# Value and output-gate projections with 512 moving columns, and half of the transposed inputs in another buffer

## The chip, the cores and the metric

The kernel runs on one core of one Trainium2 chip. The metric is device microseconds per execution: the median of three runs, beside one profiled execution whose trace is read here. A core has engines that run their own queues of instructions in order and wait for each other by semaphores: TensorE (PE, with its weight loads shown as PEld), VectorE (DVE), ScalarE (ACT), GpSimd (POOL) and SyncE (SP), which here only issues DMA transfers.

## The reference

One layer of a streaming encoder, in float32, for 2048 prompt frames (in chunks of 64 for the recurrence) and 64 sample frames that continue a running stream; model width 1024.

```
mod = silu(c) @ w_ada + b_ada                       # shift, scale, gate, twice
hn = rms(x) * (1 + sc1) + sh1
q, f, iv, og, xr, gr = split(hn @ w_in)             # six parts of 512 columns
o = hgrn2(silu(q), log(fgate(f)), 1 - fgate(f), iv) # 4 heads of 128, gated linear recurrence
o_hg = o * rsqrt(mean(o*o)) * gain * silu(og)       # og: the output gate
o_rg = rglru(conv4(xr)) * gelu(gr)                  # real-gated recurrence
x = x + g1 * (concat(o_hg, o_rg) @ w_out)
hn2 = rms(x) * (1 + sc2) + sh2
x = x + g2 * (relu(hn2 @ w_up)**2 @ w_down)         # d_ff = 4096
y = rms(x) * final_gain
```

`iv` are the values and `og` the output gate of the four HGRN2 heads. Final states are outputs too.

## The kernel before

**Blocks.** The prompt is worked in 4 blocks of 512 frames; the last block takes the 64 sample frames along (`B.last`). Activations are kept transposed (model width on the partitions) in `B.XT`, as a high part in a rounded 32-bit format and a low part with the rest; a weight tile `wt` also has a high and a low half of 1024 columns each. Each product is three matmuls: high x high, high x low, low x high.

**Weights.** A "unit" is 128 x 1024 numbers of a weight matrix. In block 0 a unit of `w_in` or `w_out` is loaded raw by SyncE, cast by ScalarE (L244), its rest is taken by VectorE or GpSimd (L245), and the split tile of 1 MB is written to memory; blocks 1 to 3 load that kept tile by GpSimd's queue (L263). `w_up` and `w_down` are split afresh in each block. All split tiles live in one pool `wp` of six slots, taken in the order of the program text; raw ones in `rawp`, of three.

**One block**, in the order of the text: the projections of head 0 (`hg_proj`, ps_in), the values (`hg_vo(B, 0)`), the gates (`hg_vo(B, 1)`), the projections of the other heads, with the recurrence of each head (`hg_chunks`: ps_dg, ps_lv, ps_kT, ps_dS, ps_o; then, in the second part, the norm, the gate and the transposes ps_oT) between them; the recurrent branch (`rg_in`, `rg_scan`, `rg_out`); the output projection (`phase_O`, ps_y); then eight groups of the MLP, up (`phase_U`, ps_u) and down. A scheduler writes the order of each engine's queue at compile time, by the rank that `sec(...)` gives a part and by its own estimate of when operands are ready. In `sec`, the last up group has rank 180, the next block's `phase_A` 182, the down group 6 185, the down group 7 195.

**hg_vo.** The activations are the stationary operand (128 frames), the weights move. For each of two halves of 256 columns, two units of 256 columns each cover the 8 slices of the model width; for each tile of 128 frames 24 matmuls sum into `ps_vo`, and ScalarE or VectorE write the result to `B.vo`. Head h reads columns 128 h to 128 h + 127 of it: ps_dS the values, L900 the gates. Value tiles of a head are needed for all four tiles of 128 frames before the head's state sums.

**phase_A** of the next block runs while the last groups of the MLP do. It spreads the frames' row scales over the partitions by four matmuls (ps_rs), copies them to an `hd` tile (L531, 512 of its 2560 columns), loads the transposed input in four quarters (`x_t`, 512 KB each), scales them with VectorE (L538), and writes XT (L539 by ScalarE, L540 by VectorE). XT has one buffer, so this waits for the last up group's matmuls. Quarters 0 and 1 live in `xap`, quarters 2 and 3 in the pool `rowp` (two buffers, tag "row").

**Down projection of blocks 1 to 3** (`phase_W`, ps_d): seven products of half-size blocks take the place of eight; the weight combinations are made on the way, from four raw tiles (`down_units`), two of them in the same pool "row":

```
r11, r21 = load_raw(w_down[u]), load_raw(w_down[u + 1])
r12, r22 = (rowp.tile([P, 1028], F32, tag="row", name="raw")[:, :D] for _ in range(2))
Q.dma_start(r12, w_down[u + 2])
Q.dma_start(r22, w_down[u + 3])
```

Four subtractions (L1036) and seven splits (L244 and L245) follow; the first two products need only r11 and r21. The left factors (gA, gS) are sums of the up result, made by VectorE in `sums_of` (L965 to L974) from an `hd` tile; each product's two results are added to accumulators by VectorE (L1086), and `combine` (L1115) puts them together after group 7. Block 0 uses the plain `phase_D0` (L1063).

The pools that the change touches: `hdp` has 2 buffers of 2560 columns, `rowp` 2, `xap` 2, `wp` 6.

Of the kernel before, what the change touches and what calls it, by code (L numbers as in the profile page):

```python
# [9 lines left out]
F32 = mybir.dt.float32  # L10
# [3 lines left out]
AF = mybir.ActivationFunctionType  # L14
# [5 lines left out]
P = 128  # L20
D = 1024
KD = 8
# [35 lines left out]
IN_UNIT = list(range(24))  # L58
# [23 lines left out]
def layout(inputs):  # L82

    a = {k: np.ascontiguousarray(v) for k, v in inputs.items()}
    d = {k: a[k] for k in ("x_prompt", "x_sample", "state_hgrn", "final_gain")}
    names = ("c_prompt", "c_sample", "b_ada", "conv_w", "conv_b", "rg_ba", "rg_bx", "rg_lambda",
             "hg_lb_logits", "hg_norm_gain", "cache_conv", "state_rglru")
    a["b_ada"] = a["b_ada"].reshape(6, D)[PARTS]
    rows = np.concatenate([a[k].reshape(-1, P) for k in names])
    small = np.zeros((P, P), np.float32)  # L90
    small[:, :len(rows)] = rows.T
    d["small"] = small

    def cols(w, n):
        return w.reshape(KD, P, -1, n).transpose(2, 1, 0, 3)

    xt = a["x_prompt"][0].reshape(-1, BLK, 4, 2, P)

    gate_w = np.zeros((P, 4, 2, P), np.float32)
    for m, nm in enumerate(("rg_wa", "rg_wx")):  # L100
        for c in range(4):
            for hf in range(2):
                sl = slice(hf * 64, hf * 64 + 64)
                gate_w[sl, c, m, sl] = a[nm][0][2 * c + hf]
    d["rg_w"] = gate_w.reshape(P, D)
    d["x_t"] = np.ascontiguousarray(xt.transpose(0, 2, 4, 3, 1)).reshape(-1, 4, P, 2 * BLK)
    win = a["w_in"][0]
    units = []
    for c in range(0, 24):
        if 8 <= c < 16:  # L110
            if c % 2 == 0:
                u = cols(win[:, c * P:(c + 2) * P], 256)[0]
                units += [u[:, 0:4].reshape(P, 1024), u[:, 4:8].reshape(P, 1024)]
        else:
            units.append(cols(win[:, c * P:(c + 1) * P], P)[0].reshape(P, 1024))
    d["w_in"] = np.stack(units)
    d["w_up"] = np.ascontiguousarray(cols(a["w_up"][0], P)).reshape(DFF // P, P, 1024)
    d["w_out"] = np.ascontiguousarray(
        a["w_out"][0].reshape(4, 2, P, 2, 512).transpose(3, 0, 2, 1, 4)).reshape(8, P, 1024)
    d["w_down"] = np.ascontiguousarray(  # L120
        a["w_down"][0].reshape(8, 2, 2, P, 2, 512).transpose(0, 4, 1, 3, 2, 5)).reshape(32, P, 1024)
    wa = a["w_ada"][0].reshape(KD, P, 6, KD, P)
    d["w_ada1"] = np.ascontiguousarray(wa[:, :, 0:2].transpose(3, 1, 0, 2, 4)).reshape(KD, P, KD, 2 * P)
    d["w_ada2"] = np.ascontiguousarray(wa[:, :, PARTS[2:]].transpose(2, 0, 1, 3, 4)).reshape(4, KD, P, D)
    d["ident"], d["masks"] = consts()
    return d
# [3 lines left out]
def hymba_step(ctx: ExitStack, tc: tile.TileContext, i: dict, o: dict):  # L130
# [335 lines left out]
    def rows(tok):  # L466


        return P if tok[2] else tok[1]
# [26 lines left out]
                          reason="late load")  # L496


    def x_load(src, n, after, row=False):
        x = rowp.tile([P, 1028], F32, tag="row", name="x_a")[:, :D] if row else xap.tile([P, D], F32, tag="xa", name="x_a")  # L500
        d = Q.dma_start(x[:n], src)
        if after is not None:
            gate(d, after)
        return x
# [10 lines left out]
    def phase_A(B, after=None):  # L515


        B.XT = Split(xtp, "xt", KD, "XT1")
        if B.last:
            n = LS  # L520
            x = x_load(xs, n, after)
            hd = hdp.tile([P, 2560], F32, tag="hd", name="hd_a")
            rs = rms_rstd(x, hd[:, :D], n)
            V.tensor_scalar(x[:n], x[:n], rs[:n, 0:1], None, op0=ALU.mult)
            norm_T(x, hd[:, 0:D], B.XT, BLK, n, 1, SC1, SH1)
        hd = hdp.tile([P, 2560], F32, tag="hd", name="hd_a")
        ps = pax.tile([P, 512], F32, tag="ax", name="ps_rs")
        for t in range(4):
            T.matmul(ps[:, t * P:(t + 1) * P], lhsT=B.rs[:, t:t + 1].to_broadcast([P, P]), rhs=ident, start=True, stop=True)
        rb = hd[:, 0:BLK]  # L530
        S.copy(rb, ps)  # L531
        for k2 in range(4):
            x = x_load(i["x_t"][B.b, k2], P, after, k2 > 1).rearrange("p (k t) -> p k t", k=2)
            for kk in range(2):
                k = 2 * k2 + kk
                sc, sh = modc[:, SC1, 0, k:k + 1], modc[:, SH1, 0, k:k + 1]
                hi, lo = (y[:, k, :BLK] for y in B.XT.p)
                V.scalar_tensor_tensor(x[:, kk], x[:, kk], sc, rb, op0=ALU.mult, op1=ALU.mult)  # L538
                S.activation(hi, x[:, kk], AF.Identity, bias=sh)  # L539
                V.scalar_tensor_tensor(lo, x[:, kk], sh, hi.bitcast(F32), op0=ALU.add, op1=ALU.subtract)  # L540
# [211 lines left out]
    def hg_vo(B, m):  # L752
        if m == 0:
            B.vo = [vop.tile([P, 2, 512], F32, tag="vo", name="vo") for _ in B.toks]
            B.rgw = vop.tile([P, 4, 2, P], F32, tag="vo", name="rgw")
            Q.dma_start(B.rgw.rearrange("p c m n -> p (c m n)"), i["rg_w"])
            if B.last:
                B.Ss = vop.tile([P, 2 * NH, P], F32, tag="vo", name="Sst_s")[:, :NH]
                Q.dma_start(B.Ss, i["state_hgrn"][0, 0].rearrange("h d v -> d h v"))
        for hf in range(2):  # L760
            c0 = (2 + m) * 512 + hf * 256
            ws = [unit(w_in, IN_UNIT[c0 // P] + u, 256, (EV if B.b else EV0)[u], "in", B.b) for u in range(2)]
            for ti, (t0, n, which, _, _) in enumerate(B.toks):
                ps = pmu.tile([P, 512], F32, tag="mu", name="ps_vo")
                ops = [(k, l, a) for k in range(KD) for l, a in passes(B.toks[ti], B.XT, k)]
                for q, (k, l, a) in enumerate(ops):
                    T.matmul(ps[:rows(B.toks[ti]), :256], lhsT=l, rhs=ws[k // 4][:, a, k % 4],  # L767
                             start=(q == 0), stop=(q == len(ops) - 1))
                dst = B.vo[ti][:n, m, hf * 256:hf * 256 + 256]
                if which:  # L770
                    halves(dst, ps[:, :256], n, which)
                    if m:
                        S.activation(ps[:n, :256], dst, AF.Sigmoid)
                        V.tensor_mul(dst, dst, ps[:n, :256])
                elif m == 0:
                    B.iv = S.copy(dst, ps[:n, :256])
                else:
                    S.activation(dst, ps[:n, :256], AF.Sigmoid)
                    B.og = V.tensor_mul(dst, dst, ps[:n, :256])

    def hg_group(B, tile_, n, C, which):
        g = Block()
# [556 lines left out]
```

## Time and profile before

| | |
|---|---|
| median of 3 runs | 2690.6 us (2690.57 to 2698.39) |
| profiled execution | 2700.03 us, span 2698.3 us |
| granted TensorE clock, mean | 0.955 |
| TensorE busy | 2493.6 us, 92% |
| VectorE busy | 1817.2 us, 67% |
| ScalarE busy | 1043.5 us, 39% |
| GpSimd busy | 188.0 us, 7% |

Shares are means over the span. Successive matmuls overlap, so a group's busy time divided by its number is longer than the distance between the starts of two matmuls; that distance is read from the timeline, as the time from the start of a row to the start of the next one divided by the number of matmuls in the row. VectorE instructions overlap by some 0.08 us in the same way.

### The profile page before, as it was taken

The page shows a single profiled execution, that of the slowest core. Times are in us where ns is not written, and L with a number is a line of the kernel's source. Part 1 is how long each engine was busy: PE and PEld are TensorE (multiplying, and loading weights), DVE is VectorE, ACT ScalarE, POOL GpSimd, SP SyncE. Part 2 cuts the span into 40 slices and gives each one's busy share as a digit, 9 for nine tenths or more (in the row PEclk, how much of TensorE's full clock was granted, in tenths as well). Part 3 has the DMA queues.
Part 4 walks back from the last instruction along what each step waited for, and adds up shares of the span by engine and source line. Part 5 has one row for each costly group of instructions (what it writes and reads, how often), then busy time and mean ns, then how long its engine had stood idle before and what let it go on. Part 6 is the DMA issues. An engine that isn't in the chain of part 4 may idle for free.

```text
span 2698.3 us, 34804 instructions
## 1 busy us (share of the span) xinstructions
PE 2493.6 (92%) x13592; PEld 2129.3 (79%) x13592; DVE 1817.2 (67%) x3267; ACT 1043.5 (39%) x1683; POOL 188.0 (7%) x245
## 2 busy tenths in 40 slices
PE   5878899999899999999799989999789998999997
PEld 4866787887797778888587878888579877998976
DVE  7676675766554656878864656778773576568787
ACT  4234152223212446445312436445411624644432
POOL 2311100000011100000001100000010110000000
PEclk8888799999999999999899999999889999999998
DMA  8563555667353542234363442234253643222223
GB/s 332 219 227 132 202 182 187 211 210 242 126 203 124 180 141 78 94 110 156 113 223 125 180 140 79 94 109 153 93 207 110 149 126 129 79 78 92 81 68 109
DMA packets 96420, 397.44 MB, mean 147 GB/s; under 512 B 14432, under 2 KB 16384, under 8 KB 79360
## 3 DMA queue, kind: packets, MB, share of 16 engines
q1 hardware_dynamic: 79696, 274.63, 29.6%
q0 software_dynamic: 16560, 120.59, 12.9%
q8 instruction: 107, 1.75, 0.3%
q14 instruction: 57, 0.47, 0.0%
HBM read 343.77 MB, written 51.41 MB: 146 GB/s over the span
## 4 chain that ended last, share of the span: by engine, by line
PE 70%; DVE 14%; issue 7%; DMA 5%; ACT 3%; POOL 1%; SPq 0%; DVEq 0%; POOLq 0%; ACTq 0%
PE ps_u L1011 24%; PE ps_d L1097 15%; PE ps_in L649 7%; PE ps_vo L767 6%; PE ps_d L1063 6%; PE ps_y L937 3%; DMA raw<-in_w_ada_dram 2%; PE ps_lv L841 2%; DVE wt L245 2%; PE ps_in L634 1%; PE ps_rg L710 1%; DVE ada_acc L333 1%; PE ps_s L1107 1%; PE ps_ada L337 1%; DMA wt<-kept_out 1%
## 5 line engine op out<-in xcount | busy, mean ns | idle before, releaser
L1011 PE MATMUL ps_u<-XT,wt 128*128 128x512 f32 (+2 forms) x4128 | 746.5, 341 | 17.1 <-ACT XT L399 5.9
L1011 PEld LDWEIGHTS ps_u<-XT,wt 128*128 128x128 f32 x4128 | 656.0, 189 | 99.4 <-ACT XT L399 7.1
L245 DVE TENSOR_TENSOR wt<-raw,wt 128x1024 fp32r<-128x1024 f32 x338 | 414.9, 1240 | 237.6 <-ACT wt L244 206.1
L244 ACT CAST wt<-raw 128x1024 fp32r<-128x1024 f32 x357 | 371.4, 1048 | 331.4 <-PE ps_d L1063 93.1
L649 PE MATMUL ps_in<-XT,wt 128*128 128x512 f32 (+1 forms) x1776 | 377.7, 363 | 12.9 <-ACT wt L244 6.6
L649 PEld LDWEIGHTS ps_in<-XT,wt 128*128 128x128 f32 x1776 | 293.0, 191 | 60.3 <-ACT wt L244 8.5
L1097 PE MATMUL ps_d<-wt,gS 128*128 128x512 f32 x1104 | 269.0, 402 | 41.0 <-ACT wt L244 30.7
L1097 PEld LDWEIGHTS ps_d<-wt,gS 128*128 128x128 f32 x1104 | 212.8, 194 | 92.8 <-ACT wt L244 32.3
L937 PE MATMUL ps_y<-wt,mix 128*128 128x512 f32 x800 | 207.1, 413 | 13.6 <-DVE hd_o L942 5.1
L1014 ACT ACTIVATE hd_u<-ps_u 128x512 f32<-128x512 f32 (+2 forms) x172 | 85.2, 498 | 344.3 <-PE ps_u L1011 341.0
L767 PE MATMUL ps_vo<-wt,XT 128*128 128x256 f32 x1600 | 212.6, 289 | 2.6 <-POOL wt L245 1.7
L767 PEld LDWEIGHTS ps_vo<-wt,XT 128*128 128x128 f32 x1600 | 201.0, 195 | 3.9 <-POOL wt L245 1.9
L1097 PE MATMUL ps_d<-wt,gA 128*128 128x512 f32 x828 | 196.9, 390 | 0.2
L937 PEld LDWEIGHTS ps_y<-wt,mix 128*128 128x128 f32 x800 | 154.8, 198 | 53.0 <-DVE hd_o L942 6.4
L1063 PE MATMUL ps_d<-wt,gt 128*128 128x512 f32 x768 | 182.2, 398 | 8.3 <-DVE acc L1068 8.3
L1097 PEld LDWEIGHTS ps_d<-wt,gA 128*128 128x128 f32 x828 | 154.7, 188 | 33.0 <-DVE wt L245 1.0
L1063 PEld LDWEIGHTS ps_d<-wt,gt 128*128 128x128 f32 x768 | 147.9, 193 | 40.1 <-DVE acc L1068 8.7
L1036 DVE TENSOR_TENSOR raw<-raw 128x1024 f32<-128x1024 f32 x92 | 113.4, 1233 | 4.3 <-DMA raw<-in_w_down_dram 2.2
L841 PEld LDWEIGHTS ps_lv<-hd_h 128*128 128x128 f32 x640 | 88.9, 211 | 24.6 <-issue 15.6
L1086 DVE TENSOR_TENSOR acc<-acc,ps_d 128x512 f32<-128x512 f32 x160 | 106.5, 680 | 1.9 <-PE ps_d L1097 0.9
L841 PE MATMUL ps_lv<-hd_h 128*128 128x64 f32 x640 | 92.3, 292 | 14.5 <-DVE hd_h L846 9.0
L1086 DVE TENSOR_TENSOR accM<-accM,ps_d 128x512 f32<-128x512 f32 x120 | 79.7, 681 | 38.5 <-PE ps_d L1097 38.1
(306 smaller groups left out, 2671.1 us busy)
## 6 DMA issues: line engine op xcount, KB each, us to landing
wt<-kept_in POOLq DMA_DIRECT2D x72, 1024.0 KB, 6.8
raw<-in_w_up_dram SPq DMA_DIRECT2D x128, 512.0 KB, 4.3
raw<-in_w_down_dram SPq DMA_DIRECT2D x128, 512.0 KB, 3.5
raw<-in_w_ada_dram SPq DMA_DIRECT2D x80, 512.0 KB, 4.8
wt<-kept_out POOLq DMA_DIRECT2D x24, 1024.0 KB, 5.2
kept_in<-wt POOLq DMA_DIRECT2D x19, 1024.0 KB, 8.8
raw<-in_w_in_dram SPq DMA_DIRECT2D x24, 512.0 KB, 5.3
x_a<-in_x_prompt_dram SPq DMA_DIRECT2D x16, 512.0 KB, 5.3
```

What stands on the lines that cost most here:

```text
L244: S.copy(wt[:, 0], raw)
L245: eng.tensor_tensor(wt[:, 1], raw, wt[:, 0].bitcast(F32), op=ALU.subtract)
L649: T.matmul(ps[:, :pn], lhsT=w[:, a, k], rhs=B.XT.p[x][:, k, p0:p0 + pn], start=(k == 0 and q == 0), stop=(k == KD - 1 and q == 2))
L767: T.matmul(ps[:rows(B.toks[ti]), :256], lhsT=l, rhs=ws[k // 4][:, a, k % 4], start=(q == 0), stop=(q == len(ops) - 1))
L841: T.matmul(ps[:C, c * C // 2:(c + 1) * C // 2].rearrange("p (b h) -> p b h", h=hs), lhsT=KS[:, c * C:c * C + C], rhs=qv[:, c * bc:(c + 1) ...
L937: T.matmul(ps[:rows(B.toks[ti])], lhsT=l, rhs=ws[k - k % 2][:, a, k % 2], start=(q == 0), stop=(q == len(ops) - 1))
L1011: T.matmul(ps[:, :pn], lhsT=w[:, a, k], rhs=B.XT.p[x][:, k, p0:p0 + pn], start=(k == 0 and q == 0), stop=(k == KD - 1 and q == 2))
L1014: S.activation(r, ps[:, :pn], AF.Relu)
L1036: V.tensor_tensor(d, x, y, op=ALU.subtract)
L1063: T.matmul(ps, lhsT=l, rhs=ws[half][c // 2][:, a, c % 2], start=(q == 0), stop=(q == len(ops) - 1))
L1086: return V.tensor_tensor(dst, dst, ps, op=ALU.add)
L1097: T.matmul(ps, lhsT=op[x][y][:, c, t * P:(t + 1) * P], rhs=w[:, a, c], start=(k == 0), stop=(k == len(ops) - 1))
```

## The change

`hg_vo` no longer goes over two halves: four units, each with 512 columns of two slices of the model width, are taken at once, and each tile of 128 frames is 24 matmuls of 512 columns into a whole `ps_vo`. The evictions are as wide. `layout` packs the units to match; their number and size stay. In `phase_A` the four quarters are asked for before the copy of the row scales, and quarters 2 and 3 go to columns 512 to 1535 and 1536 to 2559 of the `hd` tile that holds the row scales, no longer to "row".

```
     for c in range(0, 24):
         if 8 <= c < 16:
-            if c % 2 == 0:
-                u = cols(win[:, c * P:(c + 2) * P], 256)[0]
-                units += [u[:, 0:4].reshape(P, 1024), u[:, 4:8].reshape(P, 1024)]
+            if c % 4 == 0:
+                u = cols(win[:, c * P:(c + 4) * P], 512)[0]
+                units += [u[:, k:k + 2].reshape(P, 1024) for k in range(0, KD, 2)]
...
-    def x_load(src, n, after, row=False):
-        x = rowp.tile([P, 1028], F32, tag="row", name="x_a")[:, :D] if row else xap.tile([P, D], F32, tag="xa", name="x_a")
+    def x_load(src, n, after, x=None):
+        if x is None:
+            x = xap.tile([P, D], F32, tag="xa", name="x_a")
...
         rb = hd[:, 0:BLK]
+        xts = [x_load(i["x_t"][B.b, k2], P, after, hd[:, k2 * D - 1536:k2 * D - 512] if k2 > 1 else None) for k2 in range(4)]
         S.copy(rb, ps)
         for k2 in range(4):
-            x = x_load(i["x_t"][B.b, k2], P, after, k2 > 1).rearrange("p (k t) -> p k t", k=2)
+            x = xts[k2].rearrange("p (k t) -> p k t", k=2)
...
-        for hf in range(2):
-            c0 = (2 + m) * 512 + hf * 256
-            ws = [unit(w_in, IN_UNIT[c0 // P] + u, 256, (EV if B.b else EV0)[u], "in", B.b) for u in range(2)]
-            for ti, (t0, n, which, _, _) in enumerate(B.toks):
-                ps = pmu.tile([P, 512], F32, tag="mu", name="ps_vo")
-                ops = [(k, l, a) for k in range(KD) for l, a in passes(B.toks[ti], B.XT, k)]
-                for q, (k, l, a) in enumerate(ops):
-                    T.matmul(ps[:rows(B.toks[ti]), :256], lhsT=l, rhs=ws[k // 4][:, a, k % 4],
-                             start=(q == 0), stop=(q == len(ops) - 1))
-                dst = B.vo[ti][:n, m, hf * 256:hf * 256 + 256]
...
+        u0 = IN_UNIT[8 + 4 * m]
+        ws = [unit(w_in, u0 + u, 512, (EV if B.b else EV0)[u % 2], "in", B.b) for u in range(4)]
+        for ti, (t0, n, which, _, _) in enumerate(B.toks):
+            ps = pmu.tile([P, 512], F32, tag="mu", name="ps_vo")
+            ops = [(k, l, a) for k in range(KD) for l, a in passes(B.toks[ti], B.XT, k)]
+            for q, (k, l, a) in enumerate(ops):
+                T.matmul(ps[:rows(B.toks[ti])], lhsT=l, rhs=ws[k // 2][:, a, k % 2],
+                         start=(q == 0), stop=(q == len(ops) - 1))
+            dst = B.vo[ti][:n, m]
...
```

The lines left out write `dst` from `ps` as before, with 512 columns in place of 256.

## Rows read from the trace of the kernel before

**Rows 1.** The page, part 1: engine, busy us, share of the span, instructions.

```profile
PE 2493.6 (92%) x13592; PEld 2129.3 (79%) x13592; DVE 1817.2 (67%) x3267; ACT 1043.5 (39%) x1683; POOL 188.0 (7%) x245
```

**Rows 2.** TensorE's timeline from block 1 to 2.

```profile
1269.58 21.92 PE L1011 MATMUL ps_u<-XT,wt 128*128 128x512 f32 x96
1291.34 1.05 PE L529 MATMUL ps_rs<-ident,rsq 128*128 128x128 f32 x8
1292.15 5.72 PE L1097 MATMUL ps_d<-wt,gA 128*128 128x512 f32 x24
1311.68 12.51 PE L1097 MATMUL ps_d<-wt,gS 128*128 128x512 f32 x42 [13.81 <-ACT wt L244]
...
1345.64 8.33 PE L1097 MATMUL ps_d<-wt,gS 128*128 128x512 f32 x24 [3.58 <-DVE acc L1086]
...
1356.53 11.04 PE L649 MATMUL ps_in<-XT,wt 128*128 128x512 f32 x48
```

**Rows 3.** Windows: us, busy of PE, PEld, DVE, ACT, POOL, clock, DMA share, GB/s.

```profile
1269.00:1292.00 23.00, 23.00 (x106) 19.15 (x105) 8.02 (x9) 7.71 (x11) 0.00 (x0) 1.00 0.27 92
1292.00:1356.00 64.00, 45.10 (x170) 34.00 (x169) 60.08 (x79) 22.12 (x29) 2.64 (x5) 0.81 0.46 160
...
1879.00:1902.00 23.00, 23.00 (x108) 18.80 (x107) 9.98 (x20) 8.73 (x14) 0.00 (x0) 1.00 0.26 92
1902.00:1970.00 68.00, 46.02 (x175) 34.88 (x175) 62.29 (x85) 24.07 (x35) 1.85 (x4) 0.80 0.39 133
```

**Rows 4.** The page, part 5: the group of the value and gate matmuls.

```profile
L767 PE MATMUL ps_vo<-wt,XT 128*128 128x256 f32 x1600 | 212.6, 289 | 2.6 <-POOL wt L245 1.7
```

**Rows 5.** TensorE's timeline, block 1: start us, us, what, idle before.

```profile
786.69 14.88 PE L767 MATMUL ps_vo<-wt,XT 128*128 128x256 f32 x122
801.52 0.33 PE L904 MATMUL ps_oT<-ident,hd_h 128*128 128x128 f32 x1
...
810.85 7.55 PE L767 MATMUL ps_vo<-wt,XT 128*128 128x256 f32 x61
818.24 14.92 PE L649 MATMUL ps_in<-XT,wt 128*128 128x512 f32 x65
```

**Rows 6.** Timelines of TensorE and VectorE at the three block changes.

```profile
712.51 40.13 PE L1063 MATMUL ps_d<-wt,gt 128*128 128x512 f32 x168 [8.25 <-DVE acc L1068]
...
1267.93 0.68 DVE L965 TENSOR_TENSOR gS<-hd_u,gS 128x512 fp32r<-128x512 f32 x1
...
1905.21 0.42 DVE L400 TENSOR_TENSOR XT<-hd_a,XT 128x256 fp32r<-128x256 f32 x1
...
1912.38 0.74 DVE L538 SCALAR_TENSOR_TENSOR x_a<-x_a,modc,hd_a 128x512 f32<-128x512 f32 x1
...
1925.47 1.65 PE L1097 MATMUL ps_d<-wt,gS 128*128 128x512 f32 x3 [16.86 <-ACT wt L244]
```

**Rows 7.** SyncE's timeline around both changes; L1032, L1033 load r12, r22.

```profile
1250.32 3.96 SPq L501 DMA_DIRECT2D x_a<-in_x_t_dram  x2
...
1271.67 2.56 SPq L250 DMA_DIRECT2D raw<-in_w_down_dram  x3
1305.66 0.33 SPq L1032 DMA_DIRECT2D raw<-in_w_down_dram  x1
1308.84 0.33 SPq L1033 DMA_DIRECT2D raw<-in_w_down_dram  x1
...
1919.59 0.33 SPq L1032 DMA_DIRECT2D raw<-in_w_down_dram  x1
```

**Rows 8.** VectorE's groups in 1292 to 1356: count, busy us, mean ns.

```profile
L245 DVE TENSOR_TENSOR wt<-raw,wt 128x1024 fp32r<-128x1024 f32 x12 | 14.2, 1217 | 0.5 <-ACT wt L244 0.5
...
L1036 DVE TENSOR_TENSOR raw<-raw 128x1024 f32<-128x1024 f32 x8 | 9.7, 1217 | 0.0
```

**Rows 9.** Tiles x_a, then kept_in: DMA landing; then ps_vo: TensorE's waits (us, times).

```profile
DMA to landing us min/median/max: 3.5/4.3/6.4
...
DMA to landing us min/median/max: 4.8/7.0/20.1
...
  DMA wt<-kept_in: 2.1, 2
```

**Rows 10.** Tile ps_y: TensorE's waits for kept units (us, times).

```profile
  DMA wt<-kept_out: 7.7, 7
```

More of the change, by code (lines that the diff above doesn't have):

```diff
@@ L759, in hg_vo @@
                 Q.dma_start(B.Ss, i["state_hgrn"][0, 0].rearrange("h d v -> d h v"))
-        for hf in range(2):
-            c0 = (2 + m) * 512 + hf * 256
-            ws = [unit(w_in, IN_UNIT[c0 // P] + u, 256, (EV if B.b else EV0)[u], "in", B.b) for u in range(2)]
-            for ti, (t0, n, which, _, _) in enumerate(B.toks):
-                ps = pmu.tile([P, 512], F32, tag="mu", name="ps_vo")
-                ops = [(k, l, a) for k in range(KD) for l, a in passes(B.toks[ti], B.XT, k)]
-                for q, (k, l, a) in enumerate(ops):
-                    T.matmul(ps[:rows(B.toks[ti]), :256], lhsT=l, rhs=ws[k // 4][:, a, k % 4],
-                             start=(q == 0), stop=(q == len(ops) - 1))
-                dst = B.vo[ti][:n, m, hf * 256:hf * 256 + 256]
[L770 to L779, printed above, removed]
+        u0 = IN_UNIT[8 + 4 * m]
[7 more added lines that the diff above has]
+            dst = B.vo[ti][:n, m]
+            if which:
+                halves(dst, ps, n, which)
+                if m:
+                    S.activation(ps[:n], dst, AF.Sigmoid)
+                    V.tensor_mul(dst, dst, ps[:n])
+            elif m == 0:
+                B.iv = S.copy(dst, ps[:n])
+            else:
+                S.activation(dst, ps[:n], AF.Sigmoid)
+                B.og = V.tensor_mul(dst, dst, ps[:n])
     def hg_group(B, tile_, n, C, which):
```

## The prediction

> **What bounds the kernel now.** I read the page first, then TensorE's timeline, then the places where that timeline has holes. The page shows TensorE busy for 92% of the span and VectorE for 67% [rows 1]: over the whole span the matmuls are the bound, so the first question is what one matmul of this change costs, and the second is where TensorE still stands idle.
>
> For the first: in a stretch without holes, 96 matmuls of 512 columns fill the time from 1269.58 to 1291.34 [rows 2], 226.7 ns from start to start. The granted clock there is 1.00, which is 2.4 GHz [rows 3]. The value and gate projections run 1600 matmuls, nearly all with 256 columns [rows 4]; 122 of them in a row fill 786.69 to 801.52 [rows 5], 121.6 ns each. The mean durations on the page (289 ns) are no price, since neighbours overlap; the distance of starts is.
>
> For the second: the holes that this change can reach are at the two block changes where the down projection has seven products, block 1 to 2 and block 2 to 3. Right after the last up-projection group TensorE runs 24 matmuls and then stands for 13.81 us, in the later change for 16.86 us, both times until ScalarE has cast a weight tile [rows 2, 6]. The cast is not the cause. The two waiting tiles (r12, r22) are loaded by SyncE at 1305.66 and 1308.84, 34 us after the three issues of 1271.67, and at 1919.59 in the later change [rows 7]; the stall ends some 3 to 6 us after these issues. What held the loads is a buffer: they live in the two-deep pool "row", and the tiles allocated before them there are the third and fourth quarter of the next block's transposed input, loaded at 1250.32 [rows 7] and read only once the next XT may be written, that is after the last up-projection matmul at 1291.34 [rows 2].
>
> A third view keeps the gain small. In 1292 to 1356 VectorE is busy 60.08 of 64 us, in 1902 to 1970 62.29 of 68 [rows 3]: once the hole is over, splits, evictions and the next block's modulation all want VectorE, and TensorE's clock averages 0.81 and 0.80. Right before, in 1269 to 1292 and 1879 to 1902, VectorE is busy only 8.02 and 9.98 of 23 us [rows 3]. So the stretch is VectorE's as much as the late load's, and the load matters because it pushes VectorE's work from an idle stretch into a full one.
>
> **The change part by part.**
>
> *Quarter tiles out of "row".* The quarters 2 and 3 go to columns 512 to 2560 of the hd tile that already holds the row scales. r12 and r22 of group 6 then find their buffers as in any earlier group, and can be issued with the three issues of 1271.67. What moves ahead is VectorE's share of them: 4 subtractions and 5 splits, of the 8 and 12 in the stretch [rows 8], at 1.22 us each, 11.0 us. Two of the splits write weight slots that the last up-projection unit and the first product hold until about 1291 and 1295, so 7 operations, 8.5 us, are sure to have a free target in the idle 15 us before. Between 8.5 and 11.0 I take 9.5 for the change 1 to 2: the stretch of 64.4 us (1292.15 to 1356.53 [rows 2]) becomes about 55. Bounds: 0, if VectorE's written order keeps these splits behind the modulation; and the floor of TensorE, 168 matmuls at 226.7 ns = 38.1 us, which would give back 26. The value is near VectorE's limit and not near TensorE's, because 60.08 minus 11 is still 49 us of VectorE work. For 2 to 3 the stretch is as full (62.29 of 68), with the same operations and some waiting for the late tiles themselves, so I take 11. Sum: -20.5 us. At 0 to 1 nothing is gained: its hole of 8.25 us waits for VectorE [rows 6], and block 0's down projection takes no tile from "row".
>
> The four quarter loads stay four; two change their target. The hd slot comes free when the sums of group 6 are split; in the change 1 to 2 VectorE ends them at 1268.6 [rows 6], and such a load lands in 4.3 us [rows 9], so the quarters stand ready long before the modulation after 1292. In 2 to 3 the slot is first used for the sample rows, until 1905.21 + 0.42 [rows 6]; the loads then land at about 1910, while VectorE comes to the fourth of its scalings, the last of the first two quarters, at 1912.38 [rows 6]. Cost 0, covered by those; without the cover some 4 us once. Behind these issues on SyncE's queue stand only loads that today go out at 1919.59 [rows 7], so even the worst order is earlier than now.
>
> *512 columns.* Two matmuls of 121.6 ns become one of 226.7: 16.5 ns saved, 800 times, 13.2 us. Nearly all of it lies where TensorE runs without a pause [rows 5]; in block 0, where VectorE's chains set part of the pace, some is lost, and I leave that in the range. [...]
>
> *Four units before the first result.* Weight loads keep their bytes (1 MB per split unit), but a tile of results now needs four of the six slots, and units 0 to 3 are all released only in the last tile. At the border from values to gates two of the next four units are loaded ahead; the third can be issued 1.36 us into the last tile of 5.44 us (24 x 226.7) and is needed 6.8 us later, the fourth likewise. The median landing of such a load is 7.0 us, the worst 20.1 [rows 9]. So the border is just met or missed by a little. The nearest measured case is the output projection, which already holds four units in the same six slots: over all blocks it waited 7.7 us in 7 times for such loads, the value and gate projections today 2.1 us in 2 [rows 9, 10]. Phase O takes its units out of order and so frees them later; I take +4 over today, bounds 0 and +40 (three borders at 20.1 less the 6.8 that are covered), of which all beyond a few us is a rival below.
>
> *Later values.* Head 0's state sum needs its values from all four token tiles. Today half the columns, 96 matmuls at 121.6 ns, are enough, 11.7 us; then 96 at 226.7, 21.8 us: up to 10.1 us later in each block. I cost it 0: behind that point TensorE today has vo matmuls from 786.69 to 818.24 with only four transposes between [rows 5], 31.5 us of work that does not need the head. Without that cover it would be 10.1 x 4 = 40 us. The evictions halve in number and double in width, on engines with time there: 0.
>
> Sum: -20.5 - 13.2 + 4 = -29.7 us. The profiled execution took 2700.0 us (span 2698.3), which gives 2670; it was 9.4 us over the median 2690.6, and against that median it is 2661 us, 1.1% faster. About 0.3%, 8 us, is what a measurement here can tell from no change.
>
> **Rivals.**
>
> *TensorE's floor is nearly reached.* If the compiled order also brings group 7's splits forward, each stretch nears 38.1 us and gives up to 26: -52 - 13 + 4 = -61, 2630; likelier something between, 2630 to 2650. For it: VectorE's idle 15 us ahead. Against: its total in the stretch.
>
> *The freed tiles buy nothing* (the change does not do what it says): the splits stay behind the modulation in VectorE's order, and only the hole moves. Then -13.2 + 4 = -9.2, about 2681. For it: VectorE full to 94%; against: in the stretch before, it has nothing else to do.
>
> *The array's column rate is all that counts*: a 512 costs two 256s and only the buffers help, -20.5 + 4 = -16.5, 2674. Against it stand the two distances. [...]
>
> *Slower: weights arrive late.* One mechanism, the loads that wait for a slot now released in a bunch. There are four such borders in each of blocks 1 to 3 (into values, into gates, out to head 1, out to the recurrent inputs). The gains are 33.7 us, so from 2.8 us of exposed wait per border the change is no gain, and from 3.5 it is slower by over 0.3%; the whole landing of 7.0 at all twelve would give +84 - 34 = +50, 2741. For it: the border arithmetic has no slack, and in block 3 the sample heads hold a sixth slot. Against it: 7.7 us in all in the output projection.
>
> *Head 0's chain shows.* Part of the 40 us comes out, in blocks 0 and 3 above all; with 20 of it 2681, with all of it 2701.
>
> **How the numbers follow.** Forecast 0.58 (2650 to 2674); floor 0.14 (2626 to 2650); no buffer gain 0.09 (2677 to 2685); column rate 0.04 (2674); late weights 0.08 (above 2690); late chain 0.07 (2670 to 2701). Under 2682.5 lie the forecast, the floor and the column rate (0.76), some 0.04 of "no buffer gain" and 0.03 of the chain: faster 0.83. Over 2698.7 lie 0.06 of the late weights and 0.01 of the chain: slower 0.07. The rest is the same, 0.10. The range 2636 to 2684 leaves out 0.06 of the floor's case, the late weights and some 0.05 of two others, 0.19.
>
> **What would show it.** The loads of r12 and r22 at about 1275 on the old time base instead of 1305, and no hole of over 4 us after the 24 matmuls; stretch 64.4 down to about 55, with VectorE then over 85% busy; 800 vo matmuls at 227 ns; TensorE's waits for kept units in ps_vo of 4 to 8 us. I am wrong if the holes stay with another releaser, if the quarter loads become the wait of the modulation, or if ps_vo waits for weights by tens of microseconds.

## The result and the profile after

The changed kernel takes 2664.85 us (median of 4, 2663.96 to 2666.26) against 2691.66 us for the kernel before in the same session: a ratio of 0.9898, 95% interval 0.9882 to 0.9913, or 27.5 us less. Five rounds on a second chip gave 0.9890 (0.9869 to 0.9911). The forecast was 2661 us. The total was close; the two halves of the sum need a closer look.

The page of the changed kernel, part 1 (columns as in [rows 1]):

```profile
PE 2468.7 (93%) x12792; PEld 2071.5 (78%) x12792; DVE 1812.4 (68%) x3248; ACT 1026.8 (39%) x1640; POOL 191.5 (7%) x245
```

There are 800 matmuls fewer, as computed; the span falls by 36.2 us (2698.3 to 2662.1), a little more than the medians because the profiled execution of before was a long one.

**The block change 1 to 2.** TensorE's timeline after, which answers to [rows 2, 6]:

```profile
1251.22 21.92 PE L1012 MATMUL ps_u<-XT,wt 128*128 128x512 f32 x96
1272.98 1.05 PE L530 MATMUL ps_rs<-ident,rsq 128*128 128x128 f32 x8
1273.79 5.72 PE L1098 MATMUL ps_d<-wt,gA 128*128 128x512 f32 x24
1279.34 1.52 PE L1098 MATMUL ps_d<-wt,gS 128*128 128x512 f32 x6
1291.97 11.13 PE L1098 MATMUL ps_d<-wt,gS 128*128 128x512 f32 x42 [11.11 <-DVE accM L1087]
...
1316.71 7.10 PE L1098 MATMUL ps_d<-wt,gS 128*128 128x512 f32 x30 [1.38 <-DVE acc L1087]
...
1326.37 11.04 PE L651 MATMUL ps_in<-XT,wt 128*128 128x512 f32 x48
```

From the end of the last up-projection group (1251.22 + 21.92) to the next block's first matmul it is 53.2 us, where it was 65.0 (1269.58 + 21.92 to 1356.53, [rows 2]): 11.8 us less. At the change 2 to 3 the same stretch falls from 69.2 to 58.5 us, 10.7 less. TensorE's timeline at the change 2 to 3 after:

```profile
1893.89 10.84 PE L1098 MATMUL ps_d<-wt,gS 128*128 128x512 f32 x36 [11.68 <-DVE accM L1087]
...
1930.81 9.67 PE L651 MATMUL ps_in<-XT,wt 128*128 128x288 f32 x72
```

Yet there is still a hole of 11 us at each change. Only its releaser is another: no longer ScalarE's cast of a late weight, but an eviction by VectorE. SyncE's timeline shows that the loads did move; L1033 and L1034 load r12 and r22:

```profile
1234.01 0.33 SPq L1033 DMA_DIRECT2D raw<-in_w_down_dram  x1
1235.74 0.33 SPq L1034 DMA_DIRECT2D raw<-in_w_down_dram  x1
...
1253.31 2.56 SPq L250 DMA_DIRECT2D raw<-in_w_down_dram  x3
1255.92 0.90 SPq L502 DMA_DIRECT2D hd_a<-in_x_t_dram  x2
...
1270.56 0.33 SPq L1033 DMA_DIRECT2D raw<-in_w_down_dram  x1
1275.99 0.33 SPq L1034 DMA_DIRECT2D raw<-in_w_down_dram  x1
```

The first of the two pairs is group 6's. The whole program runs 18.4 us earlier here (the up-projection's last group starts at 1251.22 against 1269.58), so group 6's pair, at 1305.66 before [rows 7], now goes out 53 us earlier relative to the matmuls. The quarters 2 and 3 go out later than before and not earlier: at 1255.92, which is 1274 on the old time base, against 1250.32 [rows 7]. So it is not the earlier asking for the quarters that gains. Windows of the same stretches, columns as in [rows 3]:

```profile
1241.00:1264.00 23.00, 23.00 (x103) 19.05 (x102) 19.87 (x26) 10.86 (x15) 0.00 (x0) 1.00 0.39 138
1264.00:1319.00 55.00, 42.52 (x185) 34.58 (x184) 49.85 (x67) 22.20 (x31) 1.17 (x3) 0.91 0.27 93
1850.00:1873.00 23.00, 23.00 (x108) 18.84 (x107) 17.80 (x26) 11.92 (x17) 0.00 (x0) 1.00 0.38 126
1873.00:1932.00 59.00, 44.61 (x186) 36.26 (x187) 55.06 (x79) 20.88 (x31) 2.79 (x4) 0.86 0.41 147
```

VectorE is busy for 19.87 and 17.80 of the 23 us in which it had 8.02 and 9.98 [rows 3]. Its work moved from the full stretch into the idle one, as argued. What the hole waits for now is seen in VectorE's own timeline:

```profile
1275.88 2.07 DVE L540 SCALAR_TENSOR_TENSOR x_a<-x_a,modc,hd_a 128x512 f32<-128x512 f32 x3
...
1290.57 0.74 DVE L542 SCALAR_TENSOR_TENSOR XT<-hd_a,modc,XT 128x512 fp32r<-128x512 f32 x1
1291.23 1.28 DVE L1087 TENSOR_TENSOR accM<-accM,ps_d 128x512 f32<-128x512 f32 x2
```

The 16 modulation operations of the next block (L540, L542) stand ahead of the eviction at 1291.23 in VectorE's queue, which runs from 1275.88 on without a pause. TensorE has done the 30 matmuls ahead of the hole at 1280.9 and can go on only when this eviction is made.

**The wide projections.** The page's group of the value and gate matmuls, answering to [rows 4]:

```profile
L768 PE MATMUL ps_vo<-wt,XT 128*128 128x512 f32 x800 | 207.1, 409 | 2.5 <-POOL wt L245 1.6
```

TensorE's timeline in block 1, answering to [rows 5]:

```profile
784.07 5.72 PE L768 MATMUL ps_vo<-wt,XT 128*128 128x512 f32 x24
789.63 0.27 PE L905 MATMUL ps_oT<-ident,hd_h 128*128 128x128 f32 x1
```

The wait of tile `ps_vo` for kept units (us, times), answering to [rows 9]:

```profile
  DMA wt<-kept_in: 2.1, 2
```

The waits for kept units are what they were, 2.1 us in 2 times. The row of 24 matmuls takes 5.56 us (784.07 to 789.63), 231.7 ns each. Only its first step, behind a transpose, is much longer, 318 ns; read start by start from the trace the median is 227 ns, as predicted. Read in the same way, the 256 columns of before have 120 ns, not 121.6: their row in [rows 5] has a first step of 201 ns and a last one of 238. But the time from the first `ps_in` to the first `ps_y`, the head of a block, did not fall: 182.9, 187.5 and 188.0 us before in blocks 1 to 3, 183.7, 188.0 and 189.1 after. What fell is block 0: its first `ps_u` comes at 338.9 us after and at 355.9 before.

These starts, read from TensorE's timelines of all kernels, carry the rest of the study. In us; "first y", "first u" and "next" are the first matmul of the output projection, of the up-projection and of the next block; "head 1" to "head 3" are the heads of blocks 1 to 3 just named, not heads of the recurrence; "stretch" is from the end of the last up-projection matmul of a block to the next block's first matmul.

| kernel | block 0: first y | y to u | u to next | head 1 | head 2 | head 3 | stretch 1-2 | stretch 2-3 |
|---|---|---|---|---|---|---|---|---|
| before | 267.7 | 88.2 | 396.6 | 182.9 | 187.5 | 188.0 | 65.0 | 69.2 |
| before_again | 269.6 | 85.1 | 396.4 | 182.9 | 187.2 | 192.2 | 65.8 | 69.1 |
| rows_only | 266.7 | 91.0 | 397.5 | 182.9 | 189.7 | 189.6 | 53.5 | 59.0 |
| wide_only | 273.2 | 66.0 | 394.1 | 183.4 | 187.1 | 194.0 | 64.8 | 68.6 |
| after | 272.9 | 65.9 | 394.1 | 183.7 | 188.0 | 189.1 | 53.2 | 58.5 |
| after_again | 274.1 | 66.0 | 394.0 | 183.7 | 188.5 | 192.4 | 53.7 | 58.5 |
| p3_21 | 288.4 | 67.9 | 395.1 | 183.1 | 186.6 | 188.4 | 65.1 | 69.1 |
| four_256 | 284.0 | 68.2 | 395.7 | 187.3 | 191.5 | 195.8 | 54.2 | 58.2 |
| four_256_b123 | 275.0 | 67.8 | 395.8 | 187.6 | 191.5 | 204.6 | 53.7 | 58.5 |

Head 3 scatters by 4 us among equal kernels, so no argument rests on it.

### The profile page after: what moved, and what is told of

The parts are those of the page before. It is cut to its first block, busy times and chain, and to the rows that moved or that the text cites. A ratio compares the mean times of both kernels' runs of the same rounds, so it can differ in the third digit from the quotient of the medians.

```text
span 2662.1 us, 33130 instructions
## 1 busy us (share of the span) xinstructions
PE 2468.7 (93%) x12792; PEld 2071.5 (78%) x12792; DVE 1812.4 (68%) x3248; ACT 1026.8 (39%) x1640; POOL 191.5 (7%) x245
## 4 chain that ended last, share of the span: by engine, by line
PE 66%; DVE 15%; issue 9%; DMA 5%; ACT 4%; POOL 1%; SPq 0%; DVEq 0%; POOLq 0%; ACTq 0%
PE ps_u L1012 24%; PE ps_d L1098 14%; PE ps_in L651 7%; PE ps_d L1064 5%; PE ps_vo L768 4%; PE ps_y L938 3%; DVE wt L245 2%; PE ps_lv L842 2%; DMA raw<-in_w_ada_dram 2%; PE ps_in L636 1%; DMA wt<-kept_in 1%; PE ps_rg L712 1%; PE ps_s L1108 1%; DVE ada_acc L333 1%; DVE ada_acc L288 1%
## 5 line engine op out<-in xcount | busy, mean ns | idle before, releaser
L651 PE MATMUL ps_in<-XT,wt 128*128 128x512 f32 (+1 forms) x1776 | 376.5, 360 | 13.2 <-POOL wt L245 4.0
L1098 PE MATMUL ps_d<-wt,gS 128*128 128x512 f32 x1104 | 261.6, 395 | 27.2 <-DVE accM L1087 22.8
L768 PE MATMUL ps_vo<-wt,XT 128*128 128x512 f32 x800 | 207.1, 409 | 2.5 <-POOL wt L245 1.6
L768 PEld LDWEIGHTS ps_vo<-wt,XT 128*128 128x128 f32 x800 | 150.2, 195 | 32.3 <-POOL wt L245 1.9
L842 PEld LDWEIGHTS ps_lv<-hd_h 128*128 128x128 f32 x640 | 85.6, 204 | 27.5 <-issue 17.7
L842 PE MATMUL ps_lv<-hd_h 128*128 128x64 f32 x640 | 88.9, 285 | 13.8 <-DVE hd_h L847 11.8
```

Source lines behind the costliest of these rows:

```text
L651: T.matmul(ps[:, :pn], lhsT=w[:, a, k], rhs=B.XT.p[x][:, k, p0:p0 + pn], start=(k == 0 and q == 0), stop=(k == KD - 1 and q == 2))
L768: T.matmul(ps[:rows(B.toks[ti])], lhsT=l, rhs=ws[k // 2][:, a, k % 2], start=(q == 0), stop=(q == len(ops) - 1))
L842: T.matmul(ps[:C, c * C // 2:(c + 1) * C // 2].rearrange("p (b h) -> p b h", h=hs), lhsT=KS[:, c * C:c * C + C], rhs=qv[:, c * bc:(c + 1) ...
L1098: T.matmul(ps, lhsT=op[x][y][:, c, t * P:(t + 1) * P], rhs=w[:, a, c], start=(k == 0), stop=(k == len(ops) - 1))
```

## The experiments

The expectations number three accounts. By the first, the freed tiles shorten the two stretches, with VectorE as their limit, and the wide matmuls gain through what changes in block 0. By the second, the wide matmuls gain by their rate, alike in all four blocks. By the third, the freed tiles buy little. The later expectations say in brackets of which step they speak. Kernels timed together ran on one chip, where the kernel before took 2697 to 2701 us, so ratios are compared and not times.

**The kernel before, once more.** It tells whether the difference in block 0 belongs to the change or to one trace.

> The kernel before, unchanged, for a second trace. In the first trace of it block 0 (to the first value-block change) ended 19.5 us later than in the changed kernel's. If that is the change, block 0 ends here within 3 us of 752.5 again and the time is about 2700; if the first trace was a late one, block 0 ends near 743 and the time is about 2691.

First `ps_u` at 354.7 us, against 355.9 and, changed, 338.9; block 0 ends at 751.1 us (354.7 + 396.4), within 3 us of 752.5. The difference is the change's.

**Each half alone.** `rows_only` takes the edits of `x_load` and `phase_A`; `wide_only` takes those of `layout` and `hg_vo`.

> Only the quarter tiles go to the row scales' buffer; values and gates stay at 256 columns. Theory 1 (the buffers carry the change: the two block changes shortened by 22.5 us in the trace, and the 512 columns give little): 2691.7 - 22 = 2670, faster by 0.8%. Theory 2 (as predicted, buffers 20.5 and columns 9): 2671, and the wide part alone shows the other 9. Theory 3 (the columns carry it, through block 0): 2685 to 2692.

> Only the 512 columns in four units; the quarter tiles stay in the pool row. Theory 1: the heads of blocks 1 to 3 got 1.1, 1.0 and 2.6 us longer in the trace, so only block 0 can gain: 2684 to 2692. Theory 2: 2691.7 - 9 = 2682. Theory 3: 2675 or less.

`rows_only`: 0.9920 (0.9902 to 0.9938), 21.6 us less than before. Theory 3 falls. `wide_only`: 0.9951 (0.9932 to 0.9971), 13.2 us less, between the 9 us of theory 2 and the 16 or more of theory 3. Its trace has all of the gain in block 0, where the output projection's stage shrinks from 88.2 to 66.0 us; the heads of blocks 1 to 3 keep their length and so do the two stretches. The halves add up to 34.8 us, the whole to 27.5; the intervals of some 5 us on each allow this. TensorE's timeline of `rows_only` at the change 1 to 2 has the same new hole as the whole change:

```profile
1312.91 11.40 PE L1099 MATMUL ps_d<-wt,gS 128*128 128x512 f32 x42 [11.10 <-DVE accM L1088]
```

**The changed kernel, once more,** beside the two kernels that follow.

> The changed kernel once more, so that the kernels beside it have it on their own chip. Every theory: its ratio to the kernel before comes out as it did, between 0.987 and 0.992. If it comes out near 0.983, the gap between it and the kernel with the new block's modulation behind the evictions was in large part the chip's and not the rank's.

0.9890 (0.9869 to 0.9911), 2665.7 us. The two chips agree.

**Is block 0's gain only an order?** In the kernel before, the chain of head 3 (from `ps_dg` at 268.4 us on) runs beside the output projection, in the changed one (from 238.0) beside the recurrent gate's input projections. The order follows from ranks and from a planner's costs, which the wide matmuls alter. One number in the kernel before gives it the same order:

```
-RANK0 = dict(... p2=20, p3=26.0, gr=24, ...)
+RANK0 = dict(... p2=20, p3=21.0, gr=24, ...)
```

> The kernel before with one number changed: head 3's projection of block 0 is ranked 21 and not 26, ahead of the output gate's input at 24. No matmul, buffer or load changes. Theory 1 (the wide part gains because block 0's written order comes out with head 3's chain beside the input projections and not beside the output projection): the stretch from the first ps_y to the first ps_u of block 0 falls from 88 us to 64-68 us, its start moves back by 0-5 us, and the whole is 14-22 us shorter than before, a ratio of 0.992 to 0.995. Theory 2 (the wide part gains by the rate of 512 moving columns): within 3 us of before.

The ratio is 0.9998 (0.9981 to 1.0015). The output projection's stage falls to 67.9 us as expected, but its start moves back by 20.7 us: the starved time only changed its place. This half of theory 1 is wrong.

**Four units with 256 columns.** It keeps the changed kernel's grouping and nearly its order, and takes back the width:

```
-            for q, (k, l, a) in enumerate(ops):
-                T.matmul(ps[:rows(B.toks[ti])], lhsT=l, rhs=ws[k // 2][:, a, k % 2], ...
+            for c in (0, 256):
+                for q, (k, l, a) in enumerate(ops):
+                    T.matmul(ps[:rows(B.toks[ti]), c:c + 256],
+                             lhsT=l, rhs=ws[k // 2][:, a, k % 2, c:c + 256], ...
```

> The changed kernel with its four units for each projection kept, but every value and output-gate matmul cut into two of 256 columns. Theory 1: block 0 keeps the short output projection (66 us), and the whole is 0 to 6 us longer than the changed kernel run beside it. Theory 2: 800 pairs at 16.5 ns lose the whole 13.2 us, 3.3 us in each of the four heads.

The ratio is 0.9965 (0.9952 to 0.9977), 2686.1 against 2665.7 us for the changed kernel beside it: the width is worth 20.4 us (14 to 27 by the two intervals), more than either theory said. Heads 1 and 2 are 3.6 and 3.0 to 3.5 us longer than with 512 columns, about the 3.3 us of a quarter of 800 pairs at 16.5 ns (2.6 at the 13 ns that the single starts give); block 0 up to its first `ps_u` is 12.1 to 13.3 us longer (two traces of the changed kernel). But heads 1 and 2 are also 4.4 and 4.0 us longer than in the kernel before, whose matmuls have 256 columns as well. So four units at once cost some 4 us a head, and the width only paid that back. The groups of TensorE in head 1 (by line, with count, busy us, mean ns, and idle time with what ended it), in the kernel before:

```profile
L649 PE MATMUL ps_in<-XT,wt 128*128 128x512 f32 x384 | 97.4, 401 | 0.0
L767 PE MATMUL ps_vo<-wt,XT 128*128 128x256 f32 x384 | 49.6, 286 | 0.0
```

The same with four units and 256 columns:

```profile
L651 PE MATMUL ps_in<-XT,wt 128*128 128x512 f32 x384 | 97.8, 401 | 1.5 <-DVE vo L781 1.4
L769 PE MATMUL ps_vo<-wt,XT 128*128 128x256 f32 x384 | 50.1, 286 | 0.3 <-DMA wt<-kept_in 0.3
...
L882 PE MATMUL ps_o<-hd_h 128*128 128x128 f32 x18 | 3.7, 286 | 0.9 <-DVE hd_h L891 0.9
```

And in the changed kernel:

```profile
L651 PE MATMUL ps_in<-XT,wt 128*128 128x512 f32 x384 | 97.7, 401 | 1.6 <-DVE vo L780 1.4 <-DMA wt<-kept_in 0.2
L768 PE MATMUL ps_vo<-wt,XT 128*128 128x512 f32 x192 | 47.6, 397 | 0.0
```

The four-unit form adds 1.4 us in which a projection waits for the last gate tile to be evicted (a result tile now holds both halves until it is complete) and 0.9 us for VectorE's part of a head's chain; the sum of TensorE's idle time in head 1 goes from 0.8 to 3.5 us. The remaining 1.7 us of the 4.4 are in longer busy rows (the value group itself has 0.5 of it) and are not traced further.

**Width in block 0 alone.**

```
-            for c in (0, 256):
+            for c, w in ((0, 512),) if B.b == 0 else ((0, 256), (256, 256)):
```

> The changed kernel with 512 moving columns in block 0 alone; blocks 1 to 3 keep the four units and cut each matmul in two of 256 columns. From the run with 256 columns everywhere, whose three heads were 3.6, 3.5 and some 5 us longer than with 512 and whose block 0 was 13 us longer: this kernel is 10 to 13 us longer than the changed kernel (a ratio of 0.993 to 0.994), with block 0 as in the changed kernel. Rival (the columns matter in block 0 alone): within 3 us of the changed kernel.

0.9947 (0.9929 to 0.9964); the changed kernel on another chip had 0.9890, so about 15 us are lost. Block 0 stays short (first `ps_u` at 342.8 us), heads 1 and 2 are as long as with 256 columns everywhere. So the columns count in blocks 1 to 3 too. That is a little over the 10 to 13 us expected, with some 5 us of uncertainty on each ratio; head 3 took 204.6 us in this trace, on which no argument rests. For block 0 alone the ratios leave 5 us (0.9965 against 0.9947) and the first `ps_u` 9.5 us (352.2 against 342.8).

Block 0's difference between `four_256` and the changed kernel, 13.3 us, is four to five times what its pairs save. The value and gate stage, from its first to its last matmul, takes 90.0 and 86.0 us, which is 4.0 of it, about the direct saving; 6.5 more come between there and the first `ps_y`, and 2.3 in the output projection, where no matmul changed. Windows behind that stage in `four_256` (columns as in [rows 3]):

```profile
180.00:220.00 40.00, 36.68 (x142) 26.26 (x142) 24.67 (x32) 27.14 (x36) 8.15 (x6) 0.92 0.73 274
220.00:260.00 40.00, 33.26 (x191) 26.37 (x190) 36.53 (x85) 11.70 (x17) 7.31 (x5) 0.93 0.33 115
```

The same windows in the changed kernel:

```profile
180.00:220.00 40.00, 35.71 (x163) 26.68 (x161) 30.86 (x40) 29.69 (x39) 11.63 (x8) 1.00 0.75 284
220.00:260.00 40.00, 33.52 (x216) 25.94 (x216) 33.99 (x86) 11.64 (x19) 4.55 (x3) 0.96 0.23 80
```

The granted clock is 1.00 and 0.96 with the wide matmuls and 0.92 and 0.93 without (1.00 is 2.4 GHz, and the means mix it with 1.2). Windows from the end of the last value matmul to the first `ps_y`, of the changed kernel, then of `four_256`, then of `four_256_b123`, whose block 0 is wide too:

```profile
162.46:272.93 110.47, 93.21 (x504) 71.43 (x502) 89.52 (x182) 50.97 (x74) 18.92 (x15) 0.97 0.57 207
167.03:283.99 116.96, 97.95 (x503) 74.96 (x501) 87.66 (x181) 51.21 (x74) 18.46 (x15) 0.93 0.54 194
160.28:274.97 114.69, 95.80 (x504) 73.44 (x502) 89.59 (x182) 50.97 (x74) 19.38 (x15) 0.94 0.57 204
```

TensorE is idle for 17.3 us with the wide matmuls and 19.0 without, and busy with the same work for 93.2 and 98.0: most of the 6.5 us goes with the clock. In the third kernel, wide in block 0, the clock is 0.94 and the busy time 95.8, so the width alone does not settle the clock. What does stays open.

**The modulation behind the evictions.** If the 11 us hole is a cost, taking the 16 operations out of the evictions' way should return it.

```
-                with sec(b, 182):
+                with sec(b, 186):
                     phase_A(blocks[b + 1])
```

> The changed kernel with the next block's modulation ranked behind the down group 6 (186 in place of 182), so that the evictions of group 6 stand ahead of the modulation in VectorE's queue. Theory 1 (the hole of 11 us that is left is an eviction queued behind the modulation): the holes of 11.1, 11.7 and 8.25 us go, and the time falls by 10 to 25 us, to 2640 to 2655. Rival (VectorE's total work sets the stretch, in whatever order): the hole only moves, 2660 to 2668; or XT comes late for the next block's first projection, 2670 or more.

0.9827 (0.9810 to 0.9843); again, on another chip:

> The changed kernel with the modulation ranked 186 once more, beside the next two. Every theory: a ratio of 0.981 to 0.985 to the kernel before, and the stretches from the end of the 24 matmuls to the next block near 49.8 and 51.8 us.

0.9850 (0.9828 to 0.9872), so 11 to 19 us less than the changed kernel, in the range. The place is another than expected, though. (The 49.8 and 51.8 us of the expectations count from a `ps_rs` that this order puts 5 us after the last up-projection matmul; the stretches below count from that matmul in every kernel.) The stretches are 55.2 and 53.6 us at 1 to 2 in the two traces, and 57.2 and 57.2 at 2 to 3, against 53.2 to 53.7 and 58.5: nothing is gained at 1 to 2, and 1.3 us at 2 to 3. TensorE's timeline of the first trace shows a hole of 8 us in the place of the one of 11, with a third releaser:

```profile
1301.91 1.22 PE L1098 MATMUL ps_d<-wt,gS 128*128 128x512 f32 x2 [8.20 <-ACT wt L244]
```

The windows of the same kernel show why:

```profile
1270.00:1325.00 55.00, 44.23 (x176) 34.79 (x176) 54.45 (x76) 17.87 (x24) 3.17 (x6) 0.88 0.48 161
1868.00:1925.00 57.00, 43.55 (x191) 34.86 (x190) 54.45 (x79) 19.70 (x29) 2.79 (x4) 0.88 0.42 148
```

VectorE works 54.45 of 55 us and 54.45 of 57. The cast that ended the hole had itself waited for a subtraction of VectorE, as ScalarE's timeline shows:

```profile
1299.87 1.99 ACT L244 CAST wt<-raw 128x1024 fp32r<-128x1024 f32 x2 [0.41 <-DVE raw L1037]
```

Whatever stands last in VectorE's queue is what TensorE waits for, here by way of ScalarE. The gain is at the change 0 to 1, where the changed kernel had kept its 8.25 us hole ([rows 6]), and where VectorE is far from full. TensorE's timeline of the changed kernel there:

```profile
692.39 40.75 PE L1064 MATMUL ps_d<-wt,gt 128*128 128x512 f32 x168 [8.25 <-DVE acc L1069]
```

and its window, with VectorE busy for 30.09 of 49 us:

```profile
684.00:733.00 49.00, 40.75 (x170) 33.39 (x170) 30.09 (x48) 9.89 (x14) 2.69 (x5) 0.90 0.41 143
```

With rank 186 the timeline shows the same matmuls with no hole between them:

```profile
681.42 21.92 PE L1064 MATMUL ps_d<-wt,gt 128*128 128x512 f32 x96
703.18 1.05 PE L530 MATMUL ps_rs<-ident,rsq 128*128 128x128 f32 x8
703.99 5.72 PE L1064 MATMUL ps_d<-wt,gt 128*128 128x512 f32 x24
```

The next block's first projections already run among the rest of these matmuls, from 709.54 on, so a mark behind both is compared: from block 0's first `ps_u` to block 1's first `ps_y` it is 573.3 and 570.0 us against 577.8, 4.5 and 7.8 less. Head 2 also shortens, to 184.7 and 184.4 us; why is not traced. The spans of the profiled executions differ by 6.7 to 11.2 us, less than the ratios say.

**More work for VectorE.** If it bounds the two stretches, added work must come out.

```
                 V.scalar_tensor_tensor(lo, x[:, kk], sh, hi.bitcast(F32), op0=ALU.add, op1=ALU.subtract)
+                V.scalar_tensor_tensor(lo, x[:, kk], sh, hi.bitcast(F32), op0=ALU.add, op1=ALU.subtract)
```

> The same kernel, with the eight low parts of the modulation computed twice (the second time with the same result), so that VectorE has 8 x 0.75 = 6.0 us more to do at each block change. Theory 1 (VectorE is the bound in the stretches at the changes 1 to 2 and 2 to 3): each of the two grows by 5 to 6 us; at the change 0 to 1, where VectorE has slack, it grows by 0 to 3; in all 10 to 15 us, a ratio higher by 0.004 to 0.0055. Rival (weights on their way or TensorE's clock set these stretches): at most 2 us for each.

0.9881 (0.9862 to 0.9901), 9.7 us over `rank186_again` beside it. The stretches are 60.5 and 60.9 us: 5.3 to 6.9 longer at 1 to 2, 3.7 at 2 to 3, for some 5 us of added work at each change (VectorE is busy for 1828.2 us in all, against 1813.2). At 0 to 1, from the first `ps_u` to the next block's first `ps_y`, it is 572.8 us against 573.3 and 570.0. So the growth at 2 to 3 and the total, 9.7 us, are a little below what was expected. TensorE's timeline shows the hole longer by 4 us, with the same releaser:

```profile
1306.62 1.22 PE L1099 MATMUL ps_d<-wt,gS 128*128 128x512 f32 x2 [12.17 <-ACT wt L244]
```

That is theory 1, not the rival, whose limit was 2 us each.

**Less work for VectorE.** Rank 186, with two of the seven splits of a block's last group on GpSimd:

```
-        w22 = split_raw(r22, V)
+        w22 = split_raw(r22, G if g == 7 else V)
...
-        t2, t3, t4 = (split_raw(r, V) for r in (r22, r12, r21))
+        t2, t3, t4 = (split_raw(r, G if g == 7 and r is r12 else V) for r in (r22, r12, r21))
```

> The changed kernel with the modulation ranked 186, behind the sixth group's evictions (it measured 0.9827 of before), and with two of the seven splits of a block's last group of down weights given to GpSimd. Theory 1 (after the freed tiles VectorE is the bound in the stretch between the 24 matmuls and the next block): VectorE has 2 x 1.22 us less to do in each of the blocks 1 and 2, the two stretches of 49.8 and 51.8 us are 2 to 3 us shorter each, and the ratio falls by 0.001 to 0.002, to about 0.981. Rival (the loads or TensorE set the stretch now): no change beyond 1 us. Slower by 2 to 6 us if GpSimd's 2.5 us for a split makes a matmul wait for its weights.

0.9836 (0.9814 to 0.9858), 2650.4 us: no different from rank 186 by its intervals. The stretches are 53.9 and 55.9 us: at 2 to 3 that is 1.3 shorter than with rank 186 alone, at 1 to 2 it lies between the two traces' 55.2 and 53.6, where 2 to 3 us less were expected at each. GpSimd's group of splits between 1262 and 1318:

```profile
L245 POOL TENSOR_TENSOR wt<-raw,wt 128x1024 fp32r<-128x1024 f32 x2 | 6.7, 3344 | 358.2 <-ACT wt L244 358.2
```

VectorE's splits in the same window:

```profile
L245 DVE TENSOR_TENSOR wt<-raw,wt 128x1024 fp32r<-128x1024 f32 x7 | 10.1, 1446 | 0.0
```

GpSimd took 3.34 us for a split, and VectorE's seven own splits 1.45 us on average instead of the 1.22 of [rows 8]. That average hides one operation. The timelines of GpSimd, VectorE and TensorE have:

```profile
1303.52 2.99 POOL L245 TENSOR_TENSOR wt<-raw,wt 128x1024 fp32r<-128x1024 f32 x1 [2.86 <-ACT wt L244]
1304.79 2.81 DVE L245 TENSOR_TENSOR wt<-raw,wt 128x1024 fp32r<-128x1024 f32 x1
1300.20 13.83 PE L1098 MATMUL ps_d<-wt,gS 128*128 128x512 f32 x46 [2.56 <-POOL wt L245]
```

Six of the seven took 1.22 us, and the one that started during GpSimd's second split took 2.81. So 1.6 of the 2.4 us taken from VectorE came back in one split, and TensorE waited 2.56 us for GpSimd's first: the slower case of the expectation, in part.

## Why the prediction was right, and where it was not

**The buffers: -20.5 forecast, -21.6 measured alone, -22.5 in the two stretches.** Mechanism and size hold: loads earlier, VectorE's splits in its idle time ahead (8.02 to 19.87 us busy, 9.98 to 17.80), each stretch shorter by about 11 us. What failed is the sign that I had named for it, "no hole of over 4 us", and with it "I am wrong if the holes stay with another releaser": they stay, at 11.1 and 11.7 us, with another releaser, and the price is right all the same. I had argued that the stretch is VectorE's, and did not follow this through to the sign: where VectorE sets the length, TensorE must stand still somewhere, and the order in VectorE's queue only says where. Three runs show it: with the evictions ahead the hole moves to the splits, with some 5 us more work the stretches grow by 4 to 7; with less work one of them shrinks by 1.3 us, too little to carry weight alone. By the same token the rival of TensorE's floor (stretches near 38 us) had no way open.

**512 columns: -13.2 forecast; the step was mis-sized.** The width by itself is worth 20.4 us (14 to 27). My price for a pair was a little high: 121.6 ns is the mean of a row with two longer steps, and with single starts 120 and 227 ns apart a pair saves 13 ns, 10.4 us in all. In blocks 1 and 2 the heads gained 3.0 to 3.6 us each, somewhat over the 2.6 of that distance, so the rival of the column rate is refuted there. The Trainium skill ("TensorE: Matmul & The Clock Gate", Back-to-back issue gap) gives columns / 2.4 plus about 2.5 ns at full clock as the gap of an isolated matmul. By that gap, as an estimate, 200 pairs would save 0.5 us; the traces do not agree, with 3.0 to 3.6. For a stream with weight loads the same section names about 131 ns at 512 columns, where the rows have 226.7. In block 0, where I expected a part of the gain to be lost, the traces give 9.5 to 13 us; the pairs explain 2.6 of it and the rest stays open.

**Four units at once: +4 forecast; about +7 in sum.** That is the 20.4 less the 13.2 that `wide_only` gained, with some 8 us of uncertainty by their intervals. The place failed: no weight comes late (2.1 us of waits for kept units in `ps_vo`, as before; `ps_y` 7.8 us in 6 times, [rows 10]). Heads 1 and 2 pay some 4 us each. In head 1 the trace shows 2.3 of it, in evictions of the wider result tiles and in VectorE's part of a chain, which I had costed at 0 as "engines with time there". Block 0 gained 2.5 to 3.7 from the regrouping (352.2 against 354.7 and 355.9). So a gain set 7 us too low and a cost set 3 us too low partly met in the sum: that the total was nearer than these terms was luck.

**The rest.** Head 0's later values cost TensorE no wait that a trace shows, but they do show: VectorE's first wait for a state sum (`ps_dS`) in blocks 1 to 3 grew from 2.7, 2.7 and 5.6 us to 13.0, 7.5 and 13.0. The quarter loads, at 1255.92, were ready before the first operation on them at 1281.73; in the later change they landed at 1885.2 and 1886.5, ahead of 1887.86. The change 0 to 1 was costed at 0, and kept its hole to the hundredth, 8.25 us.

## What to carry to other kernels

When a stall goes and the work that follows is bound by another engine, look for the stall under a new releaser, and judge the edit by the length of the stretch, never by the hole; where the next part starts inside the stretch, measure to a mark behind both. An order in a queue was worth changing here where the engine that owns it has idle time (4.5 and 7.8 us at the change 0 to 1), and worth little where it is full (nothing at 1 to 2, 1.3 us at 2 to 3). Price a wider instruction together with what it holds: the result tile until the last column, the weights until the last row.

## What was not expected of the hardware

From start to start, at a granted clock of 1.00, matmuls of 256 columns lie 120 ns apart and matmuls of 512 columns 227 ns. So 256 more columns cost 107 ns, and by these two widths some 13 ns of each matmul do not depend on its columns. A row behind a transpose has one longer step (318 ns before the second of 24), which lifts its mean to 231.7. VectorE's split that started during a split of GpSimd took 2.81 us at both block changes (at 1304.79 and 1905.26) where its other splits took 1.22, and GpSimd's took 2.99 and 3.00 us against a mean of 2.50 over the rank-186 kernel: the two slowed each other. And with the wide matmuls the granted clock right behind the value and gate stage of block 0 (180 to 220 us) was 1.00 and not the 0.92 of `four_256`, in a window in which no matmul had changed.
